# A hybrid recurrent trunk in fp32: the seam before its feed-forward layer, the order in the second layer, and the last store

## The chip, the cores and the metric

The kernel runs on one core of one Trainium2 chip. The metric is the device time of one execution in microseconds, as the median of several executions. A core has five engines that the profile names: PE (TensorE, matmuls; its weight loads are the row PEld), DVE (VectorE), ACT (ScalarE), POOL (GpSimd) and SP (SyncE, which here only issues DMAs). Each engine works through its own instructions in the order in which the program was written out for it, and waits on semaphores for the others. DMAs are issued from SP's queue and from ACT's; an issue on ACT stands in the same order as ACT's arithmetic.

## The reference, cut to what matters

One layer of a trunk: a mixer (a gated linear recurrence over 2048 latent tokens behind 256 context tokens), then a feed-forward part with a convolution, then a last RMS norm. Width 1024, feed-forward width 2816, all in fp32:

```python
lat = lat + g1 * yl                                   # mixer's output projection inside yl
hl = modulate(rmsnorm(lat, norm_g[l, 1]), sh2, sc2)
lat = lat + g2 * conv_ffn(hl, ffn_w_up[l], ffn_conv_w[l], ffn_conv_b[l], ffn_w_down[l])
return rmsnorm(lat, final_g)

def conv_ffn(h, w_up, conv_w, conv_b, w_down):
    u = dwconv(h @ w_up, conv_w, conv_b)              # three taps over the positions
    gate, val = jnp.split(u, 2, axis=-1)
    return (jax.nn.silu(gate) * val) @ w_down
```

## The kernel before, in words

**Products.** Each fp32 factor is rounded into two parts, a high one (ACT copies it into the fp32r type) and a low one (DVE subtracts the high part from the source): this is `split`, lines 77 to 80, so ACT's roundings have line L78 and DVE's L79 whatever they belong to. A product of 128 columns is then three matmuls of 128x512 (high by high, high by low, low by high), lines 1065 to 1068 in the first layer of the feed-forward part, 1644 to 1646 in the second.

**The mixer** (to line 1014) fills the first half of the time. The change does not touch its instructions.

**The mixer's output** (`mixer_out`, from line 1152) walks over the 16 token tiles from the last to the first. For each it multiplies by the output weights in two halves (`residual`, L1188 to L1190), adds to the latent, takes the norm (`norm_steps`), transposes (`transpose_mod`, PE L120), scales (ACT L124) and rounds (`norm2` and `put`). Two-by-two block products are done by the Strassen-Winograd scheme with seven products, so `norm2` makes seven right factors B11, T2, T1, T3, B21, B22, T4. Tokens are in two halves of 1024. For the second half (tiles 8 to 15) the factors B11, B21, B22 stay in SBUF; all others are written to memory (`rhs_d`) by a DMA after rounding: through the two buffers of `rawp` (tag "raw") for tiles 1 to 7, and for tile 0 through `last_put`, five slices of the places that held the output weights. The stores of tiles 1 and 0 are issued on ACT's queue (L1218, L1223), the others on SP's.

**The seam.** At the end of that walk the first layer of the feed-forward part is begun on its first two column pairs (`first`): PE multiplies A11 by B11 for both pairs, A12 by B21 for the first, then the tokens of tile 0 are normed and rounded (`norm2(0, xn)`, line 1340), and A12 by B21 for the second pair and S2 by T2 for both follow. Then the pools of the mixer close and new ones open over their bytes: `wp`, a ring of 11 buffers for rounded left factors, and the working pools. T1 by S1 is the first product in them (tile `zd`), then S4 by B22, S3 by T3 and A22 by T4; two blocks of twelve matmuls each, one for each pair. The right factors T3 and T4 are loaded (`load_rhs`, L1106, SP) when their bytes are free.

**The first layer's loop** (line 1509) goes over 22 column pairs in each half of the tokens, with a list `todo` of blocks; `prepare(g)` rounds the left factor of block g (and has POOL make the sums S1, S2 and so on), nine blocks ahead (`LOOK`). All nine are asked for ahead of the first product. After each pair the taps of the convolution, the gate and the stores to memory (`Middle`) are spread over the next blocks. Results of T1 and T3 are read out of their accumulators by DVE (L1527, L1531) before the next product adds to the same bank.

**The second layer** (from line 1728) has six stages of eleven steps and a last one; in each step eight output tiles get three matmuls each. In stages 0 to 5 all eight banks accumulate over the eleven steps; at the end of a stage `phase_end` (line 1673) copies or adds all eight into SBUF, and in stages 1 to 3 the next stage goes on adding to the same banks. `ahead(s)` loads and makes the factors of the coming steps: `make_left` (three steps ahead; in stages 1 to 3 DVE adds or subtracts two loaded blocks, L1605, then ACT and DVE round: `mh` and `ml`), `make_right` (five steps ahead; where a sum is wanted DVE subtracts, L1634, then rounding into `wd`, and the sum is stored for a later stage). `later` holds the arithmetic that follows a stage (residuals, squares, the last norm), one item for each step. The last stage forms the last eight output tiles one after the other; behind each, DVE adds (L1783), ACT squares (L1661), two small DVE instructions and a power on POOL (L75) give the norm's factor, and `finish` (L1670, L1671) scales and stores two halves.

**What sets the order.** The framework writes out each engine's order by priority (the order of the program text, if nothing else is said) as its own model of the times finds the instructions ready. `tc.high_priority` moves instructions to an earlier priority; `tc.issue_after(i)` ties the instructions in its block, on i's engine alone, behind i in that engine's order. A buffer of a pool is reused when all its readers are done.

Of the kernel before, what the change touches and what calls it, by code (L numbers as in the profile page):

```python
# [45 lines left out]
def body(ctx, tc, a, out):  # L46
# [82 lines left out]

    ch = ctx.enter_context(ExitStack())  # L130
    rawp = pool_(ch, "rawp", 2)
# [930 lines left out]
    def acc_mm(o, w, r, start):  # L1062

        for k in range(4):
            pe.matmul(o, w[:, 0, k], r[:, :, 0, k], start=start and k == 0, stop=False,  # L1065
                      skip_group_check=True)
            pe.matmul(o, w[:, 0, k], r[:, :, 1, k], start=False, stop=False, skip_group_check=True)  # L1067
            pe.matmul(o, w[:, 1, k], r[:, :, 0, k], start=False, stop=k == 3, skip_group_check=True)  # L1068
# [38 lines left out]

    class Pair:
# [23 lines left out]
        def split(self, n, w=None):  # L1132
            if n in self.w:
                return
            if n == "S3" and n not in self.src:
                s3 = self.src["A21"]
                pool.tensor_tensor(s3, self.src["A11"], s3, OP.subtract)
                self.src[n] = s3
            if n == "S4" and n not in self.src:
                s2 = self.src["S2"]  # L1140
                pool.tensor_tensor(s2, self.src["A12"], s2, OP.subtract)
                self.src[n] = s2
            if w is None:
                w = wp.tile([128, 2, 4, 128], F32R, name="w", tag="w", bufs=RING)
            split(w[:, 0], w[:, 1], self.src[n])
            self.w[n] = w
# [5 lines left out]
    def mixer_out(c3):  # L1152
# [55 lines left out]
        odd, last_put = [], []  # L1208

        def put(n, t, src):  # L1210

            half, j = t // HT, t % HT // 2
            if half == 1 and n in EARLY:
                split(rhs[n][:, j, 0], rhs[n][:, j, 1], src)
                return
            if t:
                w = split_w(rawp, src, "raw", 2)
                (sp if t > 1 else act).dma_start(rhs_d[half][n][:, j], w.bitcast(F32))  # L1218
                return

            w = last_put.pop(0)
            split(w[:, 0], w[:, 1], src)
            act.dma_start(rhs_d[half][n][:, j], w.bitcast(F32))  # L1223
# [47 lines left out]
        for t in range(NT - 1, -1, -1):  # L1271
# [45 lines left out]
        pl = [place(i, [128, 4, 2, 4, 128], F32R, "w") for i in range(3)]  # L1317
        last_put.extend([pl[1][:, i] for i in (2, 3)] + [pl[2][:, i] for i in range(3)])
# [7 lines left out]
        for q, p in enumerate(first):  # L1326
            z = ps.tile([128, HJ, 128], F32, name="z", tag="y")
            acc_mm(z, p.w.pop("A11"), rhs["B11"], True)
# [29 lines left out]
    RING = NFF // 2  # L1358
# [88 lines left out]
    def right_split(s, src):  # L1447
        w = wp.tile([128, 2, 512], F32R, name="wd", tag="w", bufs=RING)
# [51 lines left out]
    rhs["T4"] = rhs_tile("T4")  # L1500
# [6 lines left out]
    for g in range(4, LOOK):  # L1507
        prepare(g)
    for g, (half, s, n, q, pairs) in enumerate(todo):
        prepare(g + LOOK)  # L1510
# [12 lines left out]
        elif n == "T1":  # L1523
# [3 lines left out]
            dve.tensor_tensor(cols(uvs[q], 1), u2s[q], z, OP.add)  # L1527
# [40 lines left out]

    sums = mk.tile([128, 2, NT], F32, name="sums")
# [23 lines left out]
    def left_split(s, width, src, **kw):  # L1593
# [6 lines left out]
        split(h, l, src)  # L1600

    def make_left(s, raw):
        ph = s // NC
        if 1 <= ph <= 3:
            dve.tensor_tensor(raw[0], raw[0], raw[1], OP.add if ph == 1 else OP.subtract)  # L1605
# [25 lines left out]
    def make_right(s, raw):  # L1631
        ph, c = divmod(s, NC)
        if len(raw) > 1:
            dve.tensor_tensor(raw[0], raw[0], raw[1], OP.subtract)  # L1634
# [38 lines left out]
    def phase_end(ph, ys):  # L1673

        for j, z in enumerate(ys):
            if ph == 0:
                act.activation(P[:, j], z, AF.Copy)
            elif ph == 1:
                act.activation(X[:, j], z, AF.Copy)  # L1679
                later.append(lambda j=j: dve.tensor_tensor(X[:, j], P[:, j], X[:, j], OP.subtract))  # L1680
            elif ph == 2:
                act.activation(V[:, j], z, AF.Copy)
                later.append(lambda j=j: residual2(2 * j, 1, V[:, j]))
            elif ph == 3:
                if j % 2 == 0:
                    st["w", j] = st["w", j + 1] = left_raw()
                w = st["w", j][:, j % 2 * 512:(j % 2 + 1) * 512]
                act.activation(w, z, AF.Copy)
                st["c22", j] = w

                def c22(j=j, w=w):
                    dve.tensor_tensor(X[:, j], X[:, j], w, OP.add)  # L1692
                    residual2(2 * j + 1, 0, X[:, j])
                    residual2(2 * j + 1, 1, w)
                    square(2 * j + 1, 1, w)
                later.append(c22)
            elif ph == 4:
                dve.tensor_tensor(P[:, j], P[:, j], z, OP.add)

                def c11(j=j):  # L1700
                    residual2(2 * j, 0, P[:, j])
                    square(2 * j, 0, P[:, j])
                later.append(c11)
            else:
                dve.tensor_tensor(X[:, j], X[:, j], z, OP.add)

                def c21(j=j):
                    square(2 * j + 1, 0, X[:, j])
                    finish(2 * j + 1, (X[:, j], st["c22", j]))
                later.append(c21)  # L1710
# [17 lines left out]
    for s in range(N):  # L1728
# [13 lines left out]
        if s >= 2:  # L1742
            ahead(s)
# [15 lines left out]
    for s in range(N, N + NC):  # L1759
        ahead(s)  # L1760

# [9 lines left out]
    for i, (j, cs) in enumerate(pieces):  # L1771
# [9 lines left out]
        if cs.start:  # L1781
            v = V[:, j]
            dve.tensor_tensor(v, v, z, OP.add)  # L1783
            square(2 * j, 1, v)
            finish(2 * j, (P[:, j], v))
# [28 lines left out]
```

## Time and profile before

| | us |
|---|---|
| median of 3 runs (lowest, highest) | 2746.97 (2746.45, 2750.19) |
| the profiled execution's own time | 2752.72 |
| its span, from the first to the last instruction | 2750.7 |
| PE busy in the span | 2705.6 |
| DVE, ACT, POOL busy | 1974.7, 1128.9, 563.3 |

The profile is of one execution. A line of its timeline has the start and the length in us, the engine, the line of the code, the operation, what it writes and reads, and in square brackets the idle time of the engine just before and what ended it. A line of the list of waits has the waiting instruction, what it waited for, the sum in us, how many times and the longest. A line of the windows has, for a stretch of time, each engine's busy time and its number of instructions, the granted clock of PE, the share of time that the DMA engines were busy and their rate. The stages of the second layer stand between these times in the span: 0 from 2315 to 2375 us, 1 to 2436, 2 to 2502, 3 to 2563, 4 to 2624, 5 to 2684, and the last one to the end.

### The profile page before, as it was taken

Reading aid. Unit: us, or ns where it says so; the run is one execution under the profiler, and the core shown is the slowest. Engines: PE = TensorE matmul, PEld = TensorE weight load, DVE = VectorE, ACT = ScalarE, POOL = GpSimd, SP = SyncE. Lnnn points to the kernel's source line nnn. Section 1 sums busy time; section 2 is a strip of 40 time slices with the busy share of each in tenths; the row PEclk is TensorE's granted clock in tenths of the full one; section 3 lists DMA queues with packets and bytes.
Section 4 is the critical chain, followed back from the end, with each engine's and each line's share of the span. In section 5 each row is a group of like instructions: output and inputs, shape, how many; then the busy total and the mean of one; then the engine's idle time right before and its main releaser. Section 6 shows DMA issues by size and latency. Waiting matters only on the chain. (4 is left out here: it accounts for less than half of the span.)

```text
span 2750.7 us, 42006 instructions
## 1 busy us (share of the span) xinstructions
PE 2705.6 (98%) x16060; PEld 2253.6 (82%) x16060; DVE 1974.7 (72%) x2791; ACT 1128.9 (41%) x1885; POOL 563.3 (20%) x885
## 2 busy tenths in 40 slices
PE   6999999999999999999998999999999999999998
PEld 4888888888888888888887888888888888877887
DVE  4756655556766766668986888776977777686886
ACT  4434443333233233335665444443444444333443
POOL 2111111111111111211111533343433440000001
PEclk9999999999999999999999999999999999999999
DMA  5313322234534443228887322227322225987663
GB/s 230 93 54 103 106 88 94 81 100 168 155 123 138 146 139 115 86 94 292 288 320 301 92 92 79 75 81 302 93 85 69 85 85 161 327 282 245 186 195 123
DMA packets 229105, 410.56 MB, mean 149 GB/s; under 512 B 29605, under 2 KB 137509, under 8 KB 225065
## 3 DMA queue, kind: packets, MB, share of 16 engines
q1 hardware_dynamic: 224584, 398.13, 43.7%
q10 hardware_dynamic: 4320, 9.77, 0.9%
q8 instruction: 126, 2.06, 0.3%
q14 instruction: 75, 0.61, 0.1%
HBM read 293.23 MB, written 114.57 MB: 148 GB/s over the span
## 5 line engine op out<-in xcount | busy, mean ns | idle before, releaser
L449 PE MATMUL z<-tok,w 128*128 128x512 f32 x1280 | 515.4, 403 | 0.0
L450 PE MATMUL z<-tok,w 128*128 128x512 f32 x1280 | 500.9, 391 | 0.4 <-DVE tok L79 0.4
L451 PE MATMUL z<-tok,w 128*128 128x512 f32 x1280 | 501.1, 391 | 0.0
L79 DVE TENSOR_TENSOR w<-raw,w 128x512 fp32r<-128x512 f32 (+1 forms) x260 | 239.7, 925 | 135.2 <-ACT w L78 131.2
L451 PEld LDWEIGHTS z<-tok,w 128*128 128x128 f32 x1280 | 240.4, 188 | 51.9
L450 PEld LDWEIGHTS z<-tok,w 128*128 128x128 f32 x1280 | 241.1, 188 | 45.9 <-DVE tok L79 1.7
L449 PEld LDWEIGHTS z<-tok,w 128*128 128x128 f32 x1280 | 240.6, 188 | 45.9 <-issue 1.7
L78 ACT ACTIVATE w<-raw 128x512 fp32r<-128x512 f32 (+1 forms) x260 | 195.9, 759 | 137.2 <-PE zd L1068 77.1
L1646 PE MATMUL y<-wd,ml 128*128 128x512 f32 x600 | 234.8, 391 | 4.1 <-DVE ml L79 4.0
L1644 PE MATMUL y<-wd,mh 128*128 128x512 f32 x600 | 234.3, 390 | 1.5 <-ACT X L1679 0.8
L1645 PE MATMUL y<-wd,mh 128*128 128x512 f32 x600 | 234.0, 390 | 0.0
L521 DVE TENSOR_TENSOR_SCAN S<-F,d 128x528 f32<-128x528 f32 (+1 forms) x80 | 91.6, 1145 | 120.5 <-ACT F L503 120.5
L79 DVE TENSOR_TENSOR w<-s,w 128x512 fp32r<-128x512 f32 x126 | 120.2, 958 | 54.3 <-ACT w L78 53.5
L75 POOL TENSOR_TENSOR rs<-rs,mhalf 128x1 f32<-128x1 f32 (+3 forms) x53 | 58.9, 1112 | 424.8 <-DVE rs L74 424.8
L1065 PE MATMUL zc<-rT,w 128*128 128x512 f32 x352 | 137.1, 390 | 1.2 <-DVE uv L1531 1.0
L1646 PEld LDWEIGHTS y<-wd,ml 128*128 128x128 f32 x600 | 113.0, 188 | 30.2 <-DVE ml L79 6.7
L1068 PE MATMUL zc<-rT,w 128*128 128x512 f32 x352 | 136.9, 389 | 0.0
L1067 PE MATMUL zc<-rT,w 128*128 128x512 f32 x352 | 136.9, 389 | 0.0
L78 ACT ACTIVATE w<-s 128x512 fp32r<-128x512 f32 x126 | 78.2, 628 | 137.5 <-POOL s L1121 80.9
L1644 PEld LDWEIGHTS y<-wd,mh 128*128 128x128 f32 x600 | 113.0, 188 | 25.8 <-ACT X L1679 1.2
L1645 PEld LDWEIGHTS y<-wd,mh 128*128 128x128 f32 x600 | 112.9, 188 | 23.5
L1065 PE MATMUL za<-rB,w 128*128 128x512 f32 x336 | 130.7, 389 | 0.0
(353 smaller groups left out, 6240.3 us busy)
## 6 DMA issues: line engine op xcount, KB each, us to landing
raw<-in_w_up_dram SPq DMA_DIRECT2D x88, 512.0 KB, 4.0
raw<-in_w_in_dram SPq DMA_DIRECT2D x80, 512.0 KB, 3.9
lr<-m SPq DMA_DIRECT2D x49, 512.0 KB, 5.7
m<-r SPq DMA_DIRECT2D x66, 256.0 KB, 4.4
spare<-in_w_ada_dram SPq DMA_DIRECT2D x32, 512.0 KB, 4.0
kq<-stash SPq DMA_DIRECT2D x15, 1024.0 KB, 7.7
og<-stash SPq DMA_DIRECT2D x30, 512.0 KB, 5.2
u<-in_w_down_dram SPq DMA_DIRECT2D x51, 256.0 KB, 4.2
```

The costliest lines, as they stand in the source:

```text
L78: i = act.activation(h, src, AF.Copy)
L79: j = dve.tensor_tensor(l, src, h.bitcast(F32), OP.subtract)
L449: pe.matmul(z, w[:, 0, k], h, start=k == 0, stop=False, skip_group_check=True)
L450: pe.matmul(z, w[:, 0, k], l, start=False, stop=False, skip_group_check=True)
L451: pe.matmul(z, w[:, 1, k], h, start=False, stop=k == KT - 1, skip_group_check=True)
L521: dve.tensor_tensor_scan(flat(S[:, d]), flat(F[:, d]), flat(d1[:, 0:ns]), 0.0, OP.mult, OP.max)
L1065: pe.matmul(o, w[:, 0, k], r[:, :, 0, k], start=start and k == 0, stop=False, skip_group_check=True)
L1067: pe.matmul(o, w[:, 0, k], r[:, :, 1, k], start=False, stop=False, skip_group_check=True)
L1068: pe.matmul(o, w[:, 1, k], r[:, :, 0, k], start=False, stop=k == 3, skip_group_check=True)
L1644: pe.matmul(z, lh, rh, start=start, stop=False, skip_group_check=True)
L1645: pe.matmul(z, lh, rl, start=False, stop=False, skip_group_check=True)
L1646: pe.matmul(z, ll, rh, start=False, stop=stop, skip_group_check=True)
```

## The change

It has four parts.

1. **The seam.** `rawp` stays open past the mixer, and its two buffers serve as two of the eleven buffers of the ring (`ring_tile`). The halves of tiles 2, 1 and 0 that go to memory get more places to be rounded in: two slices of the mixer's last turned tile, the buffer of `lp`, and for tile 0 the four slices of one place (`place0`) and `Sb`; the products of the pairs use places 2 and 3 instead of 0 and 1. The norm of tile 1 stands behind the second of the matmul groups of the last `residual`. The sums S3, S4 and S1 of both pairs are made, and S1 rounded, ahead of tile 0's norm, and that norm is tied behind the second A12 product's copy on ACT and behind the second A11 product on PE. DVE's two additions of T2's result are tied behind tile 0's roundings.
2. **The start of the loop.** Instead of nine blocks ahead of the first product, `prepare` goes up to six, and reaches nine ahead over the first blocks; on DVE the preparations stand behind the additions of the first two T1 blocks.
3. **The second layer.** `phase_end` is called for each tile behind its last product, not for all eight behind the step; the factors made in the next step are tied behind the last copy on its engine. In stages 1 to 3 L1605, in all stages L1634, and in stages 1 to 3 the items of `later` are tied on DVE behind the low part of the left factor made before (`behind_left`). No item of `later` is taken in the last step of a stage.
4. **The last store.** `last_finish` takes the place of `finish` in the last stage: the norm's weight is multiplied in while the square is summed, one small instruction goes, and DVE scales and SP stores one half while ACT scales and stores the other.

```diff
+    rawp = pool_(ctx, "rawp", 2)
     ch = ctx.enter_context(ExitStack())
-    rawp = pool_(ch, "rawp", 2)
...
+    RING = NFF // 2
+    rung = []
+    def ring_tile(shape):
+        rung.append(0)
+        if (len(rung) - 1) % RING < 2:
+            return rawp.tile(shape, F32R, name="w", tag="raw", bufs=2)
+        return wp.tile(shape, F32R, name="w", tag="w", bufs=RING - 2)
...
-            if t:
-                w = split_w(rawp, src, "raw", 2)
-                (sp if t > 1 else act).dma_start(rhs_d[half][n][:, j], w.bitcast(F32))
-                return
-            w = last_put.pop(0)
-            split(w[:, 0], w[:, 1], src)
-            act.dma_start(rhs_d[half][n][:, j], w.bitcast(F32))
+            if t == 0:
+                w = last_put.pop(0)
+            elif (t, n) in ((2, "T2"), (2, "T4")):
+                w = ghl2[:, 1, 0 if n == "T2" else 1].rearrange("p (a k) n -> p a k n", a=2)
+            elif (t, n) in ((2, "T1"), (1, "B22")):
+                w = lp.tile([128, 2, 4, 128], F32R, name="w", tag="stg", bufs=1)
+            else:
+                w = rawp.tile([128, 2, 4, 128], F32R, name="w", tag="raw", bufs=2)
+            put_split.append(split(w[:, 0], w[:, 1], src))
+            (sp if t > 1 else act).dma_start(rhs_d[half][n][:, j], w.bitcast(F32))
...
-                norm2(1, xn)
-            residual(1, lat, *g, between={KT - 1: turn} if t == NT - 1 else {})
+            residual(1, lat, *g, between={KT - 1: turn} if t == NT - 1 else
+                     {} if t else {1: lambda: norm2(1, xn)})
...
-        pl = [place(i, [128, 4, 2, 4, 128], F32R, "w") for i in range(3)]
-        last_put.extend([pl[1][:, i] for i in (2, 3)] + [pl[2][:, i] for i in range(3)])
+        pl = [place(i, [128, 4, 2, 4, 128], F32R, "w") for i in (2, 3, 0)]
+        last_put.extend(pl[2][:, i] for i in range(4))
+        last_put.append(hp.tile([128, 2, 4, 128], F32R, name="w", tag="Sb", bufs=1))
...
-            act.activation(cols(ug, 0), z, AF.Copy)
+            kept = act.activation(cols(ug, 0), z, AF.Copy).ins
             begun.append((u2, ug))
             if q == 0:
-                behind.append(tc.cur_priority)
-                norm2(0, xn)
+                for p in first:
+                    p.sums_in_place()
+                for p in first:
+                    p.split("S1")
+        behind.append(tc.cur_priority)
+        with tc.issue_after(kept), tc.issue_after(multiplied):
+            norm2(0, xn)
...
-            dve.tensor_tensor(u2, u2, z, OP.add)
-            p.sums_in_place()
+            with tc.issue_after(put_split[2 * q - 4][1]):
+                dve.tensor_tensor(u2, u2, z, OP.add)
...
-    for g in range(4, LOOK):
-        prepare(g)
+    ready, added = 4, []
     for g, (half, s, n, q, pairs) in enumerate(todo):
-        prepare(g + LOOK)
+        with ExitStack() as tied:
+            for i in added[-1:]:
+                tied.enter_context(tc.issue_after(i))
+            while ready <= min(g + LOOK, max(2 * g + 3, 5)):
+                prepare(ready)
+                ready += 1
...
+    def behind_left():
+        return tc.issue_after(made_left[-1]) if made_left else ExitStack()
...
         if 1 <= ph <= 3:
-            dve.tensor_tensor(raw[0], raw[0], raw[1], OP.add if ph == 1 else OP.subtract)
+            with behind_left():
+                dve.tensor_tensor(raw[0], raw[0], raw[1], OP.add if ph == 1 else OP.subtract)
...
         if len(raw) > 1:
-            dve.tensor_tensor(raw[0], raw[0], raw[1], OP.subtract)
+            with behind_left():
+                dve.tensor_tensor(raw[0], raw[0], raw[1], OP.subtract)
...
         if s >= 2:
-            ahead(s)
+            with ExitStack() as tied:
+                for i in ended:
+                    tied.enter_context(tc.issue_after(i))
+                ended.clear()
+                ahead(s)
...
             product(ys[j], [v[:, js] for v in l], r, c == 0 and ph in (0, 4, 5), c == NC - 1)
+            if c == NC - 1:
+                ended[:] = [phase_end(ph, j, ys[j])]
...
-        if later:
-            later.pop(0)()
-        if c == NC - 1:
-            phase_end(ph, ys)
+        if later and c < NC - 1:
+            with behind_left() if ph < 4 else ExitStack():
+                later.pop(0)()
...
+    def last_finish(t, v, p, z):
+        vg = wk.tile([128, 512], F32, name="latd", tag="latd", bufs=3)
+        ss = wk.tile([128, 1], F32, name="ssf", tag="ssf", bufs=2)
+        rs = wk.tile([128, 1], F32, name="rsf", tag="rsf", bufs=2)
+        dve.tensor_scalar(ss, sums[:, 0, t:t + 1], 1.0 / D, EPS, OP.mult, OP.add)
+        dve.tensor_tensor(p, p, st["fg"][:, 0:512], OP.mult)
+        dve.tensor_tensor(v, v, z, OP.add)
+        square(t, 1, v)
+        dve.tensor_tensor(vg, v, st["fg"][:, 512:], OP.mult)
+        dve.tensor_scalar(rs, sums[:, 1, t:t + 1], 1.0 / D, ss, OP.mult, OP.add)
+        pool.tensor_tensor(rs, rs, mhalf[:, 0:1], OP.pow)
+        dve.tensor_scalar(vg, vg, rs, None, OP.mult)
+        sp.dma_start(out[t * 128:(t + 1) * 128, 512:], vg)
+        act.activation(p, p, AF.Copy, scale=rs)
+        act.dma_start(out[t * 128:(t + 1) * 128, 0:512], p)
```

Not shown: `acc_mm` now returns its last matmul and `split` results are kept, so that others can be tied behind them; `right_split` takes its buffer from `ring_tile`; `phase_end` returns its instruction; an early allocation of T4's buffer goes.

More of the change, by code (lines that the diff above doesn't have):

```diff
@@ L1143, in split @@
             if w is None:
-                w = wp.tile([128, 2, 4, 128], F32R, name="w", tag="w", bufs=RING)
+                w = ring_tile([128, 2, 4, 128])
             split(w[:, 0], w[:, 1], self.src[n])
@@ L1447, in right_split @@
     def right_split(s, src):
-        w = wp.tile([128, 2, 512], F32R, name="wd", tag="w", bufs=RING)
+        w = ring_tile([128, 2, 512])
         split(w[:, 0], w[:, 1], src)
@@ L1526, in body @@
             uvs[q] = u_tile(wk, "v")
-            dve.tensor_tensor(cols(uvs[q], 1), u2s[q], z, OP.add)
+            i = dve.tensor_tensor(cols(uvs[q], 1), u2s[q], z, OP.add).ins
+            if g < 2:
+                added.append(i)
+            else:
+                added.clear()
         elif n == "T3":
@@ L1671, in finish @@
             sp.dma_start(out[t * 128:(t + 1) * 128, cs], v)
[L1673 to L1710, printed above, removed]
@@ new lines, in phase_end, with c22, c11, c21 @@
+    def phase_end(ph, j, z):
+        if ph == 0:
+            i = act.activation(P[:, j], z, AF.Copy)
+        elif ph == 1:
+            i = act.activation(X[:, j], z, AF.Copy)
+            later.append(lambda j=j: dve.tensor_tensor(X[:, j], P[:, j], X[:, j], OP.subtract))
+        elif ph == 2:
+            i = act.activation(V[:, j], z, AF.Copy)
+            later.append(lambda j=j: residual2(2 * j, 1, V[:, j]))
+        elif ph == 3:
+            if j % 2 == 0:
+                st["w", j] = st["w", j + 1] = left_raw()
+            w = st["w", j][:, j % 2 * 512:(j % 2 + 1) * 512]
+            i = act.activation(w, z, AF.Copy)
+            st["c22", j] = w
+            def c22(j=j, w=w):
+                dve.tensor_tensor(X[:, j], X[:, j], w, OP.add)
+                residual2(2 * j + 1, 0, X[:, j])
+                residual2(2 * j + 1, 1, w)
+                square(2 * j + 1, 1, w)
+            later.append(c22)
+        elif ph == 4:
+            i = dve.tensor_tensor(P[:, j], P[:, j], z, OP.add)
+            def c11(j=j):
+                residual2(2 * j, 0, P[:, j])
+                square(2 * j, 0, P[:, j])
+            later.append(c11)
+        else:
+            i = dve.tensor_tensor(X[:, j], X[:, j], z, OP.add)
+            def c21(j=j):
+                square(2 * j + 1, 0, X[:, j])
+                finish(2 * j + 1, (X[:, j], st["c22", j]))
+            later.append(c21)
+        return i.ins
@@ L1781, in body @@
         if cs.start:
[L1782 to L1785, printed above, removed]
+            last_finish(2 * j, V[:, j], P[:, j], z)
 def layout(x, c, ctx, c_ctx, w_ada, b_ada, norm_g, hg_w_in, hg_lb_logits, hg_gnorm, hg_w_out,
```

13 lines of the change are left out of this document (7 added, 6 removed).

## The prediction

> **What bounds the kernel now.** I read the page's first part, then PE's waits, then windows by stage, and only then the timeline at the places that these name. The page's chain of what ended last covers little of the span, and I do not lean on it.
>
> ```profile
> PE 2705.6 (98%) x16060; PEld 2253.6 (82%) x16060; DVE 1974.7 (72%) x2791; ACT 1128.9 (41%) x1885; POOL 563.3 (20%) x885
> ...
> L1065 PE MATMUL zc<-rT,w 128*128 128x512 f32 x352 | 137.1, 390 | 1.2 <-DVE uv L1531 1.0
> ```
>
> PE is the bound, and no matmul goes in this change. So only PE's idle time can be won. The windows show where it is:
>
> ```profile
> 1459.00:1516.00 57.00, 48.69 (x212) 38.85 (x211) 41.75 (x58) 31.14 (x58) 12.54 (x14) 0.94 0.70 271
> 1516.00:2315.00 799.00, 799.00 (x3526) 661.60 (x3526) 627.74 (x719) 367.85 (x508) 303.62 (x332) 1.00 0.32 105
> 2315.00:2375.00 60.00, 60.00 (x266) 49.67 (x266) 37.80 (x41) 21.45 (x30) 0.00 (x0) 1.00 0.89 299
> 2375.00:2436.00 61.00, 60.56 (x268) 49.81 (x266) 42.93 (x47) 21.07 (x29) 0.00 (x0) 1.00 0.91 311
> 2436.00:2502.00 66.00, 62.33 (x265) 50.39 (x266) 46.04 (x57) 25.84 (x39) 0.00 (x0) 0.97 0.77 248
> 2502.00:2563.00 61.00, 60.15 (x264) 48.89 (x263) 43.12 (x52) 22.33 (x32) 0.00 (x0) 1.00 0.70 227
> ```
>
> The second line is the undisturbed pace: 799 us / 3526 = 0.2266 us for a matmul. A block of twelve takes 2.72 us, a step of the second layer (24) 5.44 us, a stage 59.8 us. Stage 2 (2436 to 2502) takes 66. The seam (1459 to 1516) lacks 8.3 us of busy PE at a clock of 0.94. The loop after it is full: nothing is to be won in those 800 us.
>
> A matmul is busy for 0.39 us (the group's mean above) but takes only 0.227 of the pace, so a wait costs its idle time plus 0.16 us.
>
> **The change, part by part.**
>
> *The seam.* PE's waits between 1459 and 1516:
>
> ```profile
> PE zd L1065 <- ACT w L78: 5.6, 1, 5.6
> PE zc L1065 <- DVE uv L1531: 1.0, 1, 1.0
> PE zd L1065 <- DVE uv L1527: 1.0, 1, 1.0
> PE tp L120 <- DVE xn L1206: 0.5, 1, 0.5
> PE zc L1065 <- ACT w L78: 0.2, 1, 0.2
> ```
>
> With 0.16 each: 5.8 + 1.2 + 1.2 + 0.7 + 0.4 = 9.1 us (unrounded 9.10). The long one has a tail, as has the longest wait of stage 2. The windows of PE alone behind the two:
>
> ```profile
> 1488.90:1492.30 3.40, 3.37 (x8) 0.51 1.05 323
> 2489.30:2492.40 3.10, 3.03 (x7) 0.51 0.69 232
> ```
>
> The clock is at 0.51; eight matmuls take 3.40 us where 8 x 0.2266 = 1.81 would do: 1.59 more. Seven take 3.10 instead of 1.59: 1.51 more. The seam's stock is 9.10 + 1.59 = 10.69 us.
>
> Why does T1's first block wait? Its factor is rounded by ACT only when ACT has issued the last store of tile 0's norm:
>
> ```profile
> 1487.84 0.36 ACTq L1223 DMA_DIRECT2D rhs0T<-w  x1
> 1488.24 0.63 ACT L78 ACTIVATE w<-raw 128x512 fp32r<-128x512 f32 x1 [0.67 <-DVE w L79]
> ```
> ```profile
> 1488.93 0.80 PE L1065 MATMUL zd<-rT,w 128*128 128x512 f32 x1 [5.64 <-ACT w L78]
> ```
> ```profile
> 1496.36 1.29 DVE L1527 TENSOR_TENSOR uv<-u,zd 128x512 f32<-128x512 f32 x2 [2.55 <-DMA rhs0T<-w]
> ```
>
> PE had run dry at 1483.29. The fourth line is the next wait's cause: `uv` lies on bytes that a late half of tile 0 is still being stored from. The change rounds S1 ahead of tile 0's norm, into buffers of `rawp` that do not wait for the pools to close, S4 too can go early (its two buffers fall on place 1, which the output weights left), and the late halves move to place 0 and `Sb`, off `uv`'s bytes. So the 5.6, its tail and the 1.0 of L1527 go. The 0.5 of L1206 goes, since two matmul groups of `residual` (6 x 0.227 = 1.4 us) now stand ahead of the transposes. The last two waits come from DVE and ACT being full of roundings; fewer are now asked for at once, but the others' work is unchanged, so I keep half: 0.76 us.
>
> What is late next is T3, the first right factor that must be loaded once tile 0's norm has let go of its buffers.
>
> ```profile
> 1487.95 0.96 SPq L1106 DMA_DIRECT2D rT<-rhs1T  x2
> ```
> ```profile
> rT<-rhs1T SPq DMA_DIRECT2D x3, 2048.0 KB, 9.0
> ...
> raw<-in_w_up_dram SPq DMA_DIRECT2D x4, 512.0 KB, 12.8
> ```
> ```profile
> L78 ACT ACTIVATE w<-hm 128x512 fp32r<-128x512 f32 x6 | 3.6, 626 | 4.9 <-DVE hm L1248 2.5 <-DVE w L79 2.4
> L124 ACT ACTIVATE hm<-tp,B,A 128x128 f32<-128x128 f32 x8 | 3.1, 468 | 0.0
> ```
>
> T3's load is issued at 1487.95 and takes about 9.0 us. PE, not held up, would be dry of S2 at 1483.29 - 0.66 = 1482.6 and want T3 four blocks later, at 1493.5. On ACT, between 1475.2 and 1488.2, tile 0's norm takes 3.1 us of scaling and seven roundings, with 4.9 us idle on DVE; two roundings belong to tile 1 and now go ahead. The tie is the second A12 copy: that block ends two blocks ahead of 1482.6, at 1477.2, and the copy takes 0.6. Behind it I count 3.1 + 5 x 0.6 + five issues of 0.36 = 7.9 us: done by 1485.7. T3 then lands at 1485.8 + 9.0 = 1494.8: PE waits 1.3 us. Best, it waits 0; worst, the norm ends no sooner than before and T3 lands at 1496.95: 3.45 us and a slow clock (1.5) make 5.0. I take 1.3, since ACT's idle time is in the rows. Behind the tie on ACT stand the five roundings and five store issues, and SP's loads of T3 and T4 wait for them; behind the ties of DVE's two additions stands T1's read-out, which has 2.7 us. The loads of the next pairs' weights wait for A22's rounding, now behind the second T1 addition; their products come 8 blocks (21.8 us) after 1482.6, at 1504.4. A load asked for at about 1490 that takes 12.8 us, as in the row (behind T3 and T4), lands at 1503: covered, by little. Seam: 10.69 - 0.76 - 1.3 = **8.6 us**.
>
> *The second layer.* PE's waits between 2375 and 2684, then the order on DVE ahead of the longest:
>
> ```profile
> PE y L1646 <- DVE ml L79: 4.0, 4, 2.5
> PE y L1644 <- ACT X L1679: 0.8, 1, 0.8
> PE y L1644 <- DVE P L1698: 0.7, 1, 0.7
> ```
> ```profile
> 2487.49 0.69 DVE L1634 TENSOR_TENSOR rr<-rr,u 128x512 f32<-128x512 f32 x1 [3.77 <-DMA rr<-in_w_down_dram]
> 2488.09 1.22 DVE L79 TENSOR_TENSOR ml<-S,mh 128x1024 fp32r<-128x1024 f32 x1
> ```
> ```profile
> 2435.21 0.63 ACT L78 ACTIVATE wd<-rr 128x512 fp32r<-128x512 f32 x1 [2.41 <-DVE rr L1634]
> 2435.74 0.58 ACT L1679 ACTIVATE X<-y 128x512 f32<-128x512 f32 x1
> ```
>
> Both are the same fault: the urgent instruction stands behind one that is wanted steps later and waits for a DMA. `ml` is ready but stands behind a right factor's subtraction; the stage-end copy stands behind a right factor's rounding. The ties put L1634 and L1605 behind `ml`, and the next roundings behind the copies. Stock: 4 x 0.16 + 4.0 = 4.64, 0.96, 0.86, and the clock's 1.51: 7.97 us. One of the four `ml` waits lies in stage 3:
>
> ```profile
> PE y L1646 <- DVE ml L79: 0.7, 1, 0.7
> ```
> ```profile
> 2526.32 1.23 DVE L1605 TENSOR_TENSOR lr<-lr 128x1024 f32<-128x1024 f32 x1 [2.44 <-DMA lr<-m]
> ```
>
> There L1605 itself waits for its block, and `ml` follows from it; no order helps, so 0.87 stays. I add one new wait of a middling size (0.96): a tie also moves DMAs, since L1634 later lets the two `rr` buffers go later. The stage-end ties hold the next step's roundings until about 1 us into it, but these belong to factors wanted two steps (10.9 us) on; that covers them. Second layer: 7.97 - 0.87 - 0.96 = **6.1 us**.
>
> *The clock.* The rows: 5.64 and 2.49 us idle were each followed by some 3 us at 0.51, waits of 1.0 were not. [...]
>
> *The last store.* DVE and SP:
>
> ```profile
> 2745.16 0.16 DVE L1666 TENSOR_TENSOR ssf<-sums 128x1 f32<-128x1 f32 x1 [0.85 <-ACT sq L1661]
> 2745.35 0.15 DVE L74 TENSOR_SCALAR rsf<-ssf 128x1 f32<-128x1 f32 x1
> 2746.23 0.75 DVE L1670 SCALAR_TENSOR_TENSOR P<-P,rsf,gt 128x512 f32<-128x512 f32 x1 [0.73 <-POOL rsf L75]
> 2746.90 0.75 DVE L1670 SCALAR_TENSOR_TENSOR V<-V,rsf,gt 128x512 f32<-128x512 f32 x1
> ```
> ```profile
> 2747.67 0.33 SPq L1671 DMA_DIRECT2D out_dram<-V  x1
> ```
>
> One small step (0.19) goes, so the power ends 0.19 sooner and scaling starts at 2746.04. ACT's half takes 0.63 (as its 128x512 roundings) and is issued at about 2746.75, DVE's sooner. The last issue moves from 2747.67 by **0.9 us** (0 if ACT's store lands later than SP's did; 1.1 at best). Products and multiplications added in the earlier tiles lie under PE.
>
> **Sum.** 8.6 + 6.1 + 0.9 = 15.6 us. The profiled execution took 2752.72, 5.75 above the median; its waits are PE's own, so I take them off the median: 2746.97 - 15.6 = **2731.4**.
>
> **The rivals.**
> - *T3 sets the pace at the seam* (wait 5.0 instead of 1.3): 2735.1. For it: 9.0 us for a load, five stores ahead of it. Against: ACT's 4.9 idle us.
> - *DMA feeds stages 1 and 2* (a busy share of 0.91 and 0.77): the `ml` waits and their tail come back, and only the stage ends' 0.96 + 0.86 are won, 4.3 less: 2735.7. For it: L1634's wait is a DMA's. Against: the factor it made was not urgent. Both together: 2739.4.
> - *The ties make a chain, and it is slower.* In stages 1 to 3 L1605, `mh` on ACT, `ml`, L1634, rounding follow each other with DVE idle while ACT works. DVE's work is 46.04 / 11 = 4.19 us a step; holes of 1.05 and 0.63 and four hand-overs of 0.1 give 6.3 where all stay open. The rest of the change wins 8.6 + 0.9 + 0.86 = 10.4, and 7.1 of old waits would be swallowed, so it is slower from (33 x 5.44 + 7.1 + 10.4) / 33 = 5.97 us a step. At 6.2 (holes nearly all open): 33 x 0.23 = 7.6 above, 2754.6. Against: other work can fill a hole, and lefts are made two steps ahead.
> - *It does not do what it says:* T1's second factor shares its buffer with a half of tile 1 whose store must land first; if ACT stands there, tile 0's norm is late by as much as S1 is early. With the second layer's new waits as large as the old: 2746.
>
> **How the numbers follow.** Forecast 0.52, T3 0.17, DMA 0.13, both 0.04, chain 0.07, nothing 0.07. Own range of the likeliest: 2727.4 (all stocks won: 10.69 + 7.97 + 0.9) to 2734.5. The range 2727 to 2740 takes in the first four cases and the unknown costs. 0.2% is 5.5 us, about what a measurement of this kernel tells from no change; faster by more (under 2741.5) has 0.86, the same 0.07, slower 0.07.
>
> **What would show it.** Right: `zd` follows S2 without a gap and the clock stays at 1.0 there; stage 2 takes 60 to 61 us; `ml` stands ahead of L1634; the eight stage-end copies are 0.68 us apart. Wrong: a PE wait for `rT` or for `w` above 2 us behind 1482; waits for `ml` in stages 1 to 3 with DVE idle on ACT or `lr`; or full stretches (1516 to 2315) that take longer than before.

## The result and the profile after

| | before | after |
|---|---|---|
| median of eight runs each (lowest, highest), us | 2747.9 (2746.45, 2752.53) | 2740.65 (2738.68, 2742.91) |
| the profiled execution's own time | 2752.72 | 2739.58 |
| its span | 2750.7 | 2737.9 |

The ratio is 0.9973 with an interval of 0.9963 to 0.9982: faster by 7.3 us. The forecast was 2731.4 (15.6 us below the median shown before), the range 2727 to 2740. The direction was right, and less than half of the gain came. From profile to profile it is 13.1 us, nearly twice as much as from median to median. Two things are to be explained: what the seam did not give, and why the two comparisons differ.

The windows of the changed kernel: the seam, two stretches in it, then stages 1 to 3. The columns are those of before.

```profile
1459.00:1516.00 57.00, 52.27 (x225) 42.19 (x224) 40.57 (x58) 32.75 (x59) 12.98 (x15) 0.94 0.71 269
1488.00:1492.75 4.75, 0.86 (x5) 0.42 (x3) 4.26 (x8) 3.15 (x6) 0.00 (x0) 0.89 1.08 368
1492.70:1498.30 5.60, 5.57 (x13) 4.44 (x14) 1.76 (x4) 0.23 (x1) 0.00 (x0) 0.50 0.95 398
...
2372.00:2432.00 60.00, 60.00 (x266) 49.69 (x266) 39.50 (x44) 19.75 (x26) 0.00 (x0) 1.00 0.86 282
2432.00:2493.00 61.00, 61.00 (x271) 50.53 (x270) 46.81 (x56) 26.53 (x37) 0.00 (x0) 1.00 0.83 261
2493.00:2553.00 60.00, 60.00 (x267) 49.69 (x266) 48.68 (x61) 23.44 (x31) 0.00 (x0) 1.00 0.77 255
```

Stages 1 to 3 are now full: PE is busy from end to end at a clock of 1.00. The seam is not: it still lacks 4.7 us, its clock is still 0.94. The second line has PE at work for 0.86 us in 4.75, and the third thirteen matmuls that take 5.60 us at half the clock (0.50). PE's waits in the seam, then the longest one with what DVE and ACT did ahead of it:

```profile
PE zd L1065 <- DVE uv L1549: 3.9, 1, 3.9
PE z L1065 <- ACT w L78: 0.7, 1, 0.7
```
```profile
1492.73 0.76 PE L1065 MATMUL zd<-rB,w 128*128 128x512 f32 x1 [3.89 <-DVE uv L1549]
```
```profile
1486.17 0.68 DVE L1366 TENSOR_TENSOR u<-u,z 128x512 f32<-128x512 f32 x1
1487.11 1.29 DVE L79 TENSOR_TENSOR w<-hm,w 128x512 fp32r<-128x512 f32 x2 [0.25 <-ACT w L78]
1488.32 0.68 DVE L1366 TENSOR_TENSOR u<-u,z 128x512 f32<-128x512 f32 x1
1489.49 2.50 DVE L79 TENSOR_TENSOR w<-raw,w 128x512 fp32r<-128x512 f32 x4 [0.49 <-ACT w L78]
1491.90 1.28 DVE L1549 TENSOR_TENSOR uv<-u,zd 128x512 f32<-128x512 f32 x2
```
```profile
1478.81 0.63 ACT L78 ACTIVATE w<-raw 128x512 fp32r<-128x512 f32 x1 [3.19 <-DMA rhs0T<-w]
...
1487.83 0.95 ACTq L1237 DMA_DIRECT2D rhs0T<-w  x2
1488.83 2.19 ACT L78 ACTIVATE w<-raw 128x512 fp32r<-128x512 f32 x4 [1.23 <-DVE w L79]
```

T1 now follows S2 at once (1483.23), and B22 could begin at 1488.7. The read-out of T1's first block (L1549), for which it waits, had its data at 1486.9, when the first L1366 was done. But it stands on DVE behind four low parts (S4 and S3 of both pairs), whose high parts stand on ACT behind tile 0's last store issue. Earlier, ACT had stood for 3.19 us because S1 of the second pair found its buffer of `rawp` still being stored from; what that cost is tested below.

The second wait, for the high part of S2 of the second pair, is new. PE's order now has the transposes of tile 0 and four matmuls of S2 by T2 ahead of both A12 products, and the wait falls among these four:

```profile
1472.65 0.50 PE L1065 MATMUL z<-rT,w 128*128 128x512 f32 x1 [0.72 <-ACT w L78]
```

### The profile page after: what moved, and what is told of

It reads as the page before. It is cut to its first block, busy times and chain, and to the rows that moved or that the text cites. A ratio compares the mean times of both kernels' runs of the same rounds, so it can differ in the third digit from the quotient of the medians.

```text
span 2737.9 us, 41983 instructions
## 1 busy us (share of the span) xinstructions
PE 2702.6 (99%) x16060; PEld 2254.6 (82%) x16060; DVE 1978.3 (72%) x2799; ACT 1138.8 (42%) x1893; POOL 566.8 (21%) x885
## 4 chain that ended last, share of the span: by engine, by line
PE 94%; DMA 2%; DVE 2%; ACT 1%; issue 1%; POOL 0%; ACTq 0%; SPq 0%; POOLq 0%; DVEq 0%
PE z L449 11%; PE z L451 11%; PE z L450 11%; PE y L1678 5%; PE y L1677 5%; PE y L1679 5%; PE zc L1067 3%; PE zc L1068 3%; PE zc L1065 3%; PE zd L1065 3%; PE zd L1067 3%; PE zd L1068 3%; PE za L1067 3%; PE za L1065 3%; PE za L1068 3%; PE kv L678 2%
## 5 line engine op out<-in xcount | busy, mean ns | idle before, releaser
L1678 PE MATMUL y<-w,mh 128*128 128x512 f32 x600 | 233.5, 389 | 0.3 <-DVE w L79 0.3
L1679 PE MATMUL y<-w,ml 128*128 128x512 f32 x600 | 233.4, 389 | 0.0
L1677 PE MATMUL y<-w,mh 128*128 128x512 f32 x600 | 233.2, 389 | 0.0
L1678 PEld LDWEIGHTS y<-w,mh 128*128 128x128 f32 x600 | 112.6, 188 | 24.0 <-DVE w L79 0.7
L1679 PEld LDWEIGHTS y<-w,ml 128*128 128x128 f32 x600 | 112.6, 188 | 23.5
L1677 PEld LDWEIGHTS y<-w,mh 128*128 128x128 f32 x600 | 112.6, 188 | 23.4 <-ACT w L78 0.3
```

The lines of the kernel that those rows point to most:

```text
L1677: pe.matmul(z, lh, rh, start=start, stop=False, skip_group_check=True)
L1678: pe.matmul(z, lh, rl, start=False, stop=False, skip_group_check=True)
L1679: pe.matmul(z, ll, rh, start=False, stop=stop, skip_group_check=True)
```

## The experiments

To compare executions I use four stretches between starts of PE's matmuls in each trace: the seam (first product of the column pairs to the first of the loop's next pairs, `z` to `za`), the loop from there, the second layer (its first matmul to its last), and the tail (from there to the start of the last instruction). Each row is one execution. All are in us.

| kernel | seam | loop | second layer | tail |
|---|---|---|---|---|
| before | 49.45 | 799.68 | 428.16 | 7.41 |
| `before_again` | 49.56 | 799.68 | 425.10 | 7.43 |
| `seam_alone` | 46.83 | 799.72 | 422.71 | 7.42 |
| `last_alone` | 49.08 | 799.68 | 421.98 | 6.90 |
| `second_alone` | 49.17 | 799.68 | 420.75 | 7.46 |
| after | 46.86 | 799.68 | 419.37 | 6.90 |
| `after_again` | 46.02 | 799.85 | 419.87 | 6.90 |
| `readout_first` | 41.31 | 801.05 | 419.62 | 6.90 |
| `readout_again` | 41.88 | 801.71 | 420.63 | 6.90 |
| `free_slot` | 52.63 | 799.68 | 419.25 | 6.90 |
| `both_mended` | 49.53 | 801.58 | 421.68 | 6.90 |
| `late_s1` | 46.15 | 800.55 | 419.87 | 6.90 |
| `ends_alone` | 41.42 | 801.40 | 424.05 | 6.91 |
| `ties_alone` | 41.29 | 801.64 | 420.52 | 6.91 |

**The parts alone, and before once more.** `second_alone` is the kernel before with part 3 of the diff, `seam_alone` with parts 1 and 2, `last_alone` with part 4 (`last_finish` for `finish`); `before_again` is the kernel before. In short:

```diff
 second_alone
+            if c == NC - 1:
+                ended[:] = [phase_end(ph, j, ys[j])]
 seam_alone
+        return rawp.tile(shape, F32R, name="w", tag="raw", bufs=2)
+            while ready <= min(g + LOOK, max(2 * g + 3, 5)):
 last_alone
-            finish(2 * j, (P[:, j], v))
+            last_finish(2 * j, V[:, j], P[:, j], z)
```

> The kernel before with part 3 alone (phase_end tile by tile, the ties in the second layer). Theory A: the waits of the second layer in the kernel before are not the same in every execution. The profiled one lost 8.9 us there and stood 4.8 above the median of eight, so in the median part 3 wins about 8.8 - 4.8 = 4 us (ratio about 0.9985). Rival B: these waits are in every execution; part 3 wins its 8.8 us in the median too (0.9968), and the seam must then lose about 2. In its own trace both expect under 1 us of waits in the second layer and the old seam of 10.7.

> The kernel before with parts 1 and 2 alone. Theory A: the median falls by 2.6 to 3.5 us, what the two traces show from the last residual to the first block of the loop (ratio about 0.9989); its trace, which has the second layer of before, shows there another sum of waits than 8.9 (3 to 7). Rival B: no gain or a loss of up to 2 us (1.000 to 1.0007), with 8.9 of waits in the second layer once more. Both expect the 3.9 us wait for T1's read-out again.

> The kernel before with part 4 alone. The traces of before and after have 7.41 and 6.90 us from the last matmul's start to the end: 0.5 less, where the prediction had 0.9. In the median this is too small for the interval (0.9998, by either 0.5 or 0.9); the trace is to show 6.9. Theory A: waits in its second layer, which is that of before, sum to something else than 8.9; rival B: 8.9 again.

> The kernel before, profiled a second time. Theory A: the seam's waits are the same 10.7 us, those of the second layer are not: 3 to 7 us instead of 8.9, and where the 2.5 us wait of stage 2 is missing or under 1.5, the matmuls at half pace behind it are missing too. Rival B: the same waits at the same places to within 0.3 us each.

Measured against 2747.86 of before: `second_alone` 2744.26 (ratio 0.9988, 0.9979 to 0.9997), `seam_alone` 2744.22 (0.9987, 0.9978 to 0.9996), `last_alone` 2745.44 (0.9993, 0.9985 to 1.0002: not told from nothing). `before_again` took 2748.28 in its one run. PE's waits in the second layer of the three executions that have it as before, in the order `before_again`, `seam_alone`, `last_alone`:

```profile
PE y L1646 <- DVE ml L79: 3.1, 4, 1.0
PE y L1644 <- ACT X L1679: 1.3, 1, 1.3
```
```profile
PE y L1672 <- DVE ml L79: 1.9, 3, 0.8
PE y L1670 <- ACT X L1705: 0.4, 1, 0.4
```
```profile
PE y L1646 <- DVE ml L79: 1.6, 2, 1.0
PE y L1644 <- ACT X L1679: 0.4, 1, 0.4
```

The profile shown before had 4.0 us for `ml`, with one wait of 2.5 and seven matmuls at a clock of 0.51 behind it. None of these three has a wait of that size, and `before_again` has a clock of 1.00 over stage 2 (2435 to 2502 us), where the first profile had 0.97. The same subtraction (L1634), for which DVE stood 3.77 us on a DMA in the first profile, stood shorter in the second:

```profile
2485.62 0.69 DVE L1634 TENSOR_TENSOR rr<-rr,u 128x512 f32<-128x512 f32 x1 [2.47 <-DMA rr<-in_w_down_dram]
```

In the four executions it stood 3.77, 2.47, 2.03 and 2.47 us, and PE's wait for the `ml` behind it was 2.49, 1.05, 0.53 and 1.01. With the same code the second layer takes 428.16, 425.10, 422.71 and 421.98 us, 424.5 on average, while the seam of before repeats within 0.5. Theory A holds, rival B does not. With part 3 whole, in eight executions, it takes 419.25 to 421.68, on average 420.1: the part is worth 4.4 us in the mean, and 8.8 only against the first profile.

**The read-out first.** In the changed kernel, S4's low parts go behind the first of T1's read-outs and S3's behind the second, where A22's stood already:

```diff
-        for g in range(4):
+        for g in range(2):
             prepare(g)
-    ready, added = 4, []
+    ready, added = 2, []
...
-            while ready <= min(g + LOOK, max(2 * g + 3, 5)):
+            while ready <= min(g + LOOK, 2 * g + (3 if g > 1 else 1)):
```

> The changed kernel again, on the chip of the next three, with a second profile. Both theories: 2740.7 within 1.5, 8.0 us of waits and slow matmuls in the seam, 0.6 to 2 in the second layer.

> The changed kernel with one order turned round: the factors S4, S3 and A22 of the first two pairs are no longer prepared ahead of T1's read-outs; on DVE S4's low parts stand behind the first read-out, S3's and A22's behind the second. Theory: the 3.9 us wait is DVE's order, four low parts in front of a ready read-out. Then B22's first block waits only for S4's high part on ACT (1489.4 against 1488.5) and its low part (0.4 later): 1.7 us with the 0.16 for each wait, no matmuls at half pace, 6.8 - 1.7 = 5.1 us less: 2735.6. Rival, ACT sets it (its slot wait of 3.19 us makes all that follows late): the read-out goes early but the wait moves whole to S4's rounding, at least 3 us of idle stay and the clock still drops: 2739 to 2741.

`after_again` 2739.73 (2739.21 to 2740.92), `readout_first` **2736.17** (2734.44 to 2737.41); before it 2746.61 (ratio 0.9959, 0.9947 to 0.9972). The orders of PE, ACT and SP are those of the changed kernel. DVE in `readout_first`, then PE's waits and the window of the seam:

```profile
1487.18 0.68 DVE L1366 TENSOR_TENSOR u<-u,z 128x512 f32<-128x512 f32 x1
1487.78 0.68 DVE L1549 TENSOR_TENSOR uv<-u,zd 128x512 f32<-128x512 f32 x1
1488.38 1.28 DVE L79 TENSOR_TENSOR w<-raw,w 128x512 fp32r<-128x512 f32 x2
1489.58 0.68 DVE L1549 TENSOR_TENSOR uv<-u,zd 128x512 f32<-128x512 f32 x1
1490.18 2.49 DVE L79 TENSOR_TENSOR w<-raw,w 128x512 fp32r<-128x512 f32 x4
```
```profile
PE zb L1068 <- DVE w L79: 1.0, 1, 1.0
PE zd L1065 <- DVE uv L1549: 1.0, 1, 1.0
...
```
```profile
1459.00:1516.00 57.00, 54.13 (x244) 43.51 (x243) 44.97 (x61) 34.85 (x62) 14.73 (x17) 1.00 0.68 262
```

The 3.9 us wait is 1.0, the clock stays at 1.00, and the seam takes 41.31 for 46.86. The loop is longer by 1.4, of which 1.0 is a new wait (`zb`), and gives some of it back: the time falls by 3.6 us of the 5.1 expected, and the ranges of the two do not meet. The rival (ACT alone) is out.

**The buffer without a pending store.** `free_slot` is the changed kernel with the T3 half of tile 1 kept out of `rawp`; `both_mended` has the read-out first as well.

```diff
-            elif (t, n) in ((2, "T2"), (2, "T4")):
-                w = ghl2[:, 1, 0 if n == "T2" else 1]...
+            elif (t, n) in ((2, "T2"), (2, "T4"), (1, "T3")):
+                w = ghl2[:, 1, 1 if n == "T4" else 0]...
```

> The changed kernel with the T3 half of tile 1 rounded in a slice of the turned tile (where T2 of tile 2 was) and not in a buffer of rawp, so that S1 of the second pair finds a buffer without a pending store. DVE's order stays. Theory: ACT's 3.19 us wait goes, tile 0's norm ends about 3 us sooner, S4's and S3's roundings too, and the read-out comes at about 1488.7 in place of 1491.9: under 1 us of wait, no slow matmuls, 5.9 us less: 2734.8. Rival, DVE's order alone sets it: the four low parts still stand ahead and the wait stays above 2.5 us with slow matmuls behind it: 2738 or more. A second rival: T3's store is issued later and T3's load with it, and PE waits for T3 instead (rT in the waits).

> Both edits, the free buffer and the read-out first. Theory: the wait of B22's first block goes whole, with its tail: 6.8 us less, 2733.9, and the seam keeps about 1.3 us of waits (transposes, A12). Rival: the next late thing takes their place, T3's load or the new pairs' weights, which are asked for no sooner: 2736 or more with a wait for rT or for w.

2745.19 and 2745.09 (ratios 0.9996, 0.9987 to 1.0004, and 0.9993, 0.9984 to 1.0002): the whole gain is lost. The theory's own place came out nearly as told in `free_slot` (0.9 us of wait), but its next places did not. The edit also moved more than a buffer: ACT issues that half's store later, and PE's order has both A12 products ahead of S2 again, without the wait of 0.72 us. So it does not measure the stall on `rawp` alone. Its waits, the instructions of ACT and DVE behind the long one, and its loads:

```profile
PE zc L1065 <- issue: 9.2, 1, 9.2
PE zd L1065 <- DVE uv L1549: 0.9, 1, 0.9
...
```
```profile
1499.33 1.15 ACT L78 ACTIVATE w<-raw 128x512 fp32r<-128x512 f32 x2 [13.06 <-DMA rhs0T<-w]
```
```profile
1499.99 1.30 DVE L79 TENSOR_TENSOR w<-raw,w 128x512 fp32r<-128x512 f32 x2 [11.55 <-ACT w L78]
...
1507.59 0.68 DVE L1557 TENSOR_TENSOR uv<-uv,zc 128x512 f32<-128x512 f32 x1
```
```profile
1473.41 2.67 SPq L1108 DMA_DIRECT2D rT<-rhs1T  x2
```
```profile
rhs0T<-w ACTq DMA_DIRECT2D x3, 512.0 KB, 15.9
```

The new place lies on bytes that T1 is loaded into: T1's load was issued only at 1473.41, behind that half's store (1470.59), where the changed kernel has 1466.88, and T3's load followed within 2.7 us. Tile 0's stores, issued 3.1 us sooner (16.4 us behind the first product `z` for 19.5), now followed within 7 us of the 2 MB loads of both T1 and T3, where in the changed kernel these are issued 18 and 7 us ahead; they took 15.9 us to land. A22's buffers are on their bytes; ACT stood on them for 13.06 us, DVE on ACT, and T3's read-out (L1557), which PE needed, stood on DVE behind that. The list of waits names "issue" for it; only the order on DVE shows the cause.

**S1 rounded later.** The same stall of ACT removed without moving a load:

```diff
-                for p in first:
-                    p.split("S1")
+                first[0].split("S1")
...
             norm2(0, xn)
+        with tc.issue_after(put_split[-4][0]):
+            first[1].split("S1")
```

> The changed kernel (old order of the read-out) with S1 of the second pair rounded behind tile 0's halves on ACT, not ahead of its norm, so that ACT does not stand 3.2 us on rawp's pending store and no load is moved. Theory, the slot wait is the second cause: tile 0's norm ends 2.9 us sooner, the read-out comes at about 1489.0 for 1491.9, under 1.2 us of wait and no slow matmuls: 5.5 us less than the changed kernel, about 2734.5. Rival, the stores: issued 2.9 us sooner they fall into T3's and T4's loads, land at 1495 or later, and A22's rounding waits for their bytes as in the run with the free buffer (a wait for zc of 2 us or more): 2738 or more. What the free buffer lost 9 us to would then be the stores alone and not T1's late load.

2739.43 (2737.46 to 2744.66; ratio 0.9972, 0.9961 to 0.9982), the time of the changed kernel. The theory missed its size: the norm's tie waits for the second A12 product, so its scaling began 3.8 us ahead of T1's first matmul (1478.19 and 1482.03) instead of 2.9 (1480.30 and 1483.23): 0.9 us sooner, not 2.9.

```profile
PE zc L1065 <- issue: 1.8, 1, 1.8
PE zd L1065 <- DVE uv L1550: 1.6, 1, 1.6
PE zd L1065 <- ACT w L78: 1.5, 1, 1.5
...
PE za L1068 <- DVE w L79: 0.6, 1, 0.6
```

The waits account for its seam without matmuls at half pace: 46.15 less 5.8 for the five waits in it and 5 x 0.16 leaves 39.55 us, for 39.56 in `readout_again`, which had a clock of 1.00 behind its wait. But four waits of 0.6 to 1.8 us take the place of one: S1 comes late itself (1.5), the read-out still stands behind four low parts (1.6), and A22's rounding started only at 1495.33, after 5.56 idle us on ACT (1.8 for `zc`). The rival priced it rightly. For the last wait the timeline names only "issue", as ACT's releaser too, but the store issued at 1486.08 took 9.2 us and so landed at 1495.3, just ahead of that rounding, as the stores of `free_slot` did:

```profile
rhs0T<-w ACTq DMA_DIRECT2D x1, 512.0 KB, 9.2
```

**What in part 3 carries it.** On `readout_first`: `ends_alone` without the ties behind the left factor's low part, `ties_alone` with `phase_end` for all eight tiles behind the step again, and so without the ties behind its last copy and with `later` in a stage's last step.

```diff
 ends_alone
-        return tc.issue_after(made_left[-1]) if made_left else ExitStack()
+        return ExitStack()
 ties_alone
-            if c == NC - 1:
-                ended[:] = [phase_end(ph, j, ys[j])]
...
-        if later and c < NC - 1:
+        if later:
...
+        if c == NC - 1:
+            for j in range(HT):
+                phase_end(ph, j, ys[j])
```

> The kernel with the read-out first once more, as the base of the next two and to make its time firmer: 2736.2 within 1.5, with 1.1 us for the read-out's wait and no matmuls at half pace in the seam.

> The kernel with the read-out first, part 3 without the ties behind the left factor's low part; phase_end stays tile by tile with its ties. Theory: the ties are what removed the waits for ml; without them 3 to 5 such waits come back, which sum to 2.4 to 6.2 us (what the four executions without ties had): 2738.5 to 2742. Rival: the tile-by-tile end moved the work so that the ties are idle; no more than one wait for ml, 2736 to 2737.

> The kernel with the read-out first, part 3 with the ties behind the left factor's low part, but phase_end again for all eight tiles behind the step. Theory: no wait for ml in stages 1 to 3; at the end of stage 1 a wait of 0.6 to 1.5 us for X comes back, which the tile-by-tile end did not reliably remove either (0.3 to 2.1 us in four of six executions that have it): 2736 to 2738, not to be told from the base. Rival: the tile-by-tile end holds the gain: waits for ml or X of over 2.5 us, 2739 or more.

`readout_again` 2737.09 (ratio 0.9958, 0.9945 to 0.9972), `ends_alone` 2739.04 (0.9968, 0.9955 to 0.9980), `ties_alone` 2736.34 (0.9956, 0.9944 to 0.9969). PE's waits in the second layer, `ends_alone`, then `ties_alone`:

```profile
PE y L1677 <- ACT mh L78: 1.3, 1, 1.3
PE y L1679 <- DVE ml L79: 1.0, 2, 0.8
```
```profile
PE y L1677 <- ACT X L1711: 0.6, 1, 0.6
...
```

Without the ties the left factors come late again: two waits for `ml` and one for `mh`, where three to five for `ml` were told, and 424.05 us for the layer, more than in any of the eight executions with part 3 whole. With the ties and the old end it takes 420.52, as with both. So the traces say that the ties carry part 3; they are one execution each, and the times alone do not tell `ends_alone` from its base (2735.61 to 2744.88 against 2735.36 to 2738.07). The tile-by-tile end shows no gain: PE still waits for X, 0.2 to 1.8 us in all, in five of the eight executions that have it, as in `second_alone`.

```profile
PE y L1651 <- ACT X L1685: 0.8, 2, 0.6
```

## Why the prediction was wrong, step by step

- **The bound** was right: the loop takes 799.68 us in both profiles, and all that moved was PE's idle time and its half-speed tails.
- **The seam, 8.6 forecast, 2.6 in the profiles** (49.45 to 46.86; 0.36 more from the transposes' wait ahead of it). The waits of 5.6 and 1.0 for `w` and `uv` went, as said. The step that failed is "behind the ties of DVE's two additions stands T1's read-out, which has 2.7 us". The read-out stood also behind four low parts that DVE got from ACT only after tile 0's last store issue: the ties of part 2 hold on DVE only the seventh prepared factor (A22) and those after it, not S4 and S3, and S4, which "can go early", was rounded only at 1488.83. So the read-out came 3.89 us late and cost 0.16 + 3.89 + 2.65 for thirteen slow matmuls, 6.7 us. A new wait of 0.72 us (0.9 with the 0.16) for S2's high part, which the sum does not have, took a little more. With the read-out in front, seam and loop together take 842.36 us in place of 846.54.
- **"Done by 1485.7"** for tile 0's norm failed too: the last issue came at 1488.43, where before had 1487.84, though T1 began 5.7 us sooner. Two things held it. The stall of 3.19 us on `rawp`'s buffer delayed the norm's scaling by 0.9 us, as `late_s1` shows; for the rest of the stall the tie behind the second A12 product would have held it anyway. And that product came later than "two blocks ahead" of the end of S2: four of S2's 24 matmuls stand in front of it, so it ends 20 matmuls (4.5 us) ahead of T1 instead of 5.4. The stall is the mechanism of the last rival, in the place that it named; but the norm was not late by as much as S1 was early. What the stall alone cost stays open: in `late_s1` it is gone, but S1 of the second pair is itself late, and the time is the same (2739.43).
- **T3** cost nothing. Its load was issued at 1477.93, ahead of the norm; only T4's waited for the norm's end (1488.47). The forecast put both behind it.

```profile
1477.93 0.32 SPq L1108 DMA_DIRECT2D rT<-rhs1T  x1
```
```profile
1488.47 0.32 SPq L1108 DMA_DIRECT2D rT<-rhs1T  x1
```

- **The second layer, 6.1 forecast**: 8.8 from profile to profile, 4.4 in the mean of the executions, 3.6 as the part's own median. The mechanism was right for `ml`, and in the profile more than right: the wait in stage 3 that I kept (0.87) went too, and of the new wait of 0.96 there came 0.3. For the stage ends (0.96 and 0.86) it is not shown.
- **The sum** failed at "its waits are PE's own, so I take them off the median". The execution stood 5.75 us above the median largely because of just such waits: its second layer was 428.16 us, against 422 to 425 in three other executions of the same code. (Another 1.5 us lie ahead of the seam: the first product `z` starts at 1465.91, in `before_again` at 1464.44.) Waits that only some executions have cannot all be taken off the median. This makes most of the difference between 13.1 and 7.3.
- **The last store**, 0.9 forecast: the last issue comes 3.53 us after the last matmul's start for 4.47, 0.94 sooner, as worked out. The end comes only 0.5 sooner (6.90 for 7.41, and the same in `last_alone`): behind the issue of the last store, from ACT's queue, the execution runs for 3.4 us, behind that from SP's, in the kernel before, 2.9. The bound named this ("0 if ACT's store lands later"). Whether the queue makes the difference was not tested.

```profile
2730.90 0.39 PE L1679 MATMUL y<-w,ml 128*128 128x512 f32 x1
...
2734.43 0.34 ACTq L1814 DMA_DIRECT2D out_dram<-P  x1
```

- **The other rivals**: T3, the DMA feed and the chain of ties did not come; the stages take 60 to 61 us with PE full.

Together, in the mean: 0.4 (transposes) + 2.6 + 4.4 + 0.5 = 7.9 us, within the measured 4.9 to 10.2 (the interval of the ratio).

## What to carry to other kernels

When a wait is removed, list what is queued in front of the next urgent instruction on its engine, each with the engine that feeds it, and not only the tie that you add: here the read-out was ready and stood behind four roundings wanted later, and putting it first gave 3.6 us more than the change itself (2736.17, and 2737.09 when measured again). Before a profile's waits are taken off a median, see how far that execution stands from it, and take a second profile of the same code: here the wait that hung on a DMA's landing varied (0.5 to 2.5 us for the same `ml`), and those that hung on an order repeated (5.64 us in each of four executions with the old seam, 3.9 to 4.1 in three with the new). A buffer moved to free an engine has bytes that something else is waiting for (in `free_slot` T1's load, issued at 1473.41 for 1466.88).

## What the runs showed of the hardware that was not expected

The stretch at half the clock behind one and the same wait varied. After 5.6 us idle at the same place, before had eight matmuls in 3.40 us at 0.51; `before_again`:

```profile
1487.40:1493.85 6.45, 6.40 (x15) 4.97 (x16) 4.91 (x8) 3.64 (x8) 0.00 (x0) 0.51 1.05 384
```

Fifteen in 6.45 us; what sets the length is not shown. Nor did slow matmuls come only behind the long waits. The two waits of 0.98 us in the seam of before, 15 us apart, had none behind them (clock 1.00 from 1496 to 1502 us and from 1502 to 1516), but in `ends_alone` two waits of 1.25 and 0.78 us, 1.5 us apart, were followed by ten matmuls at 0.52:

```profile
2473.44 0.50 PE L1677 MATMUL y<-w,mh 128*128 128x512 f32 x1 [1.25 <-ACT mh L78]
...
2474.96 0.50 PE L1679 MATMUL y<-w,ml 128*128 128x512 f32 x1 [0.78 <-DVE ml L79]
```
```profile
2475.20:2478.70 3.50, 3.50 (x10) 2.69 (x10) 1.98 (x4) 1.68 (x3) 0.00 (x0) 0.52 0.64 200
```

And a 512 KB store from ACT's queue that took 3.9 us to land in the changed kernel (the median of four, with three 2 MB loads issued between 1466.9 and 1488.5) took 15.9 in `free_slot` (the median of three), where three 2 MB loads were issued between 1473.4 and 1483.7.

```profile
rhs0T<-w ACTq DMA_DIRECT2D x4, 512.0 KB, 3.9
```
